# Hybrid encoder layer on one core: loads and stores moved behind the turns, one product moved ahead of some values, the end planned anew

## The chip, the cores and the metric

The kernel runs on one core of one Trainium2 chip. The metric is the time of the whole launch in microseconds, taken on the device. Engines are named as the profile names them: PE is TensorE, PEld its weight loads, DVE VectorE, ACT ScalarE, POOL GpSimd, SP SyncE, which here only issues DMAs. A "q" behind an engine's name (SPq) means its instruction queue: a DMA's row there lasts as long as the queue was held by issuing it, not as long as the transfer.

## What is computed

One encoder layer for 4096 tokens of width 1024, in float32. Cut to what matters:

```python
def reference(x, ...):                       # x: (1, 4096, 1024)
    h = rmsnorm(x, pre_norm_g)
    proj = h @ w_in                          # 1024 -> 2304
    q, k, v, g_a, u_p, g_p = split(proj)     # 8 query heads, 2 key heads of 64
    a = banded_attention(q, k, v, rel_bias, sink) * silu(g_a)
    p = multiscale_pool(u_p, pool_w, pool_scale) * silu(g_p)
    mixed = concatenate([a, p]) @ w_out      # 1024 -> 1024
    return x + rmsnorm(mixed, post_norm_g)

def banded_attention(...):   # blocks of 128 queries, each sees 3 blocks of keys
    s = q . k * scale + bias, masked to |i-j| <= 128
    p = exp(s - m) / (sum(exp(s - m)) + exp(sink - m))
    return p . v
```

## The kernel before

Every float32 number is carried as two float16 (a high part and the rest), so a product of two matrices is three products of halves. Large products are made with seven half-size products in place of eight, and with sums of quarters before and behind them. The names p1 to p7, S1 to S4, s1 to s4 and OT1 to OT4 stand for these.

**First stage** (until about 490 us of the profiled execution). Passes m = 0 to 7 over tiles of 512 tokens. Each makes the gates and the pooling path, and writes to DRAM what the second stage reads: the normed x in halves (`x_scr`), sums of its quarters (`y_scr`), the attention gates (`ga_scr`), the pooled values (`yp_scr`) and weights. `cast` makes a high part on ACT and a rest on DVE. `x_loads` brings the rows of x of a later pass for their squares. `q_pair` folds and scales query weights, with a small matmul for their norm (`pair_norm`).

**Second stage.** 32 blocks b of 128 tokens, in 16 units u of two blocks, run from 31 down to 0. A pass m takes the units ua = 16 - 2m and ub = 15 - 2m, and with them the projections for the units that follow. For each block and each half of its heads:

- `scores` (PE): queries times keys, into the two score banks.
- `softmax`: `logits` (DVE), `exps` (ACT), `sinks`, `denominators` (DVE), `probs` (ACT, the high halves), `rests` (DVE, the low halves into `pn`).
- `turn` (SP): one transposing DMA, `pt<-pn`.
- `values` (PE, function `attend` plans it): probabilities times values. It runs 18 matmuls on the first half of the heads and 18 on the second, each waiting for its own turn.

Between these PE makes the products of the other parts: `do_kv` (keys and values), `q_product` p1 to p7 (queries), and for the output `product` by way of `mix_p1` to `mix_p7`. Behind the output products come `add`, `square`, `gain`, `mean`, `rescale`, then `add_x`, which GpSimd issues as a DMA that adds x in DRAM onto the finished tile `mo`, and `store_sum`, which SP issues as soon as that DMA has landed (`out<-mo`).

**The order is planned.** Each step is put into a list with a due time (`due(t, fn, ...)`), `now[0]` counts PE's time in products, and the list is sorted by due time at the end. The due times thus only set the order in which each engine gets its instructions; each engine then works through its own in that order and waits where it has to. `visit(b, half)` plans the scores and the softmax, with the turn 7.8 us behind the softmax's start (all starts are kept in `starts`). `settled(plan)` goes over the list once more and moves steps on DVE and ACT to places inside a softmax where they do not delay it: its `spans` are (from, to, new place, how many at most), measured from a start. The end, blocks 3 to 0, is written out by hand with times `at_(t, ...)` from z on.

**x in SBUF.** `load_x(m, name)` brings 1 MB into one of three slots. X and W are the two halves of the pass's tokens, Y and Z the sums. W of a pass takes the slot of X, the next pass's X the slot of Y, the next Y the slot of Z, and Z the slot of the pass before's W. X is read by p1, p2 and a `do_kv`, Y by p5 and p6, Z by p3 and p7, W by p4 and a `do_kv`.

One pass m > 1 before the change, in PE's order (8 visits, each with scores; the turns follow some 9 us behind):

```
visit(2ua+1,0)  mix_p5 mix_p1 mix_p3  values(2ua+2)
visit(2ua+1,1)  mix_p2 p1 p6
visit(2ua,0)    p2 mix_p6             values(2ua+1)
visit(2ua,1)    p5 p3 mix_p4 mix_p7
visit(2ub+1,0)  mix_p5 mix_p1 mix_p3  values(2ua)
visit(2ub+1,1)  do_kv(ub-1) mix_p2
visit(2ub,0)    p7 mix_p6 mix_p4      values(2ub+1)
visit(2ub,1)    p4 do_kv(ub-2) mix_p7
```

In the last pass `mix_p4` and what follows stand behind p4.

Of the kernel before, what the change touches and what calls it, by code (L numbers as in the profile page):

```python
# [70 lines left out]
def hybrid_layer(ctx: ExitStack, tc, io, out):  # L71
# [82 lines left out]
    with ExitStack() as actx:  # L154
# [1475 lines left out]

    def settled(entries):
# [5 lines left out]
        for t, n, fn, args in sorted(entries, key=lambda s: s[:2]):  # L1637
            if fn in on_dve + on_act + others:
                spans = ()
                if fn in (gain11, q_join3):  # L1640
# [3 lines left out]
                elif fn is rescale:  # L1644
                    spans = ((-0.6, 6.4, 6.4, 99),)
                elif fn is store_sum:
                    spans = ()
                elif fn in on_act:
                    spans = ((0.75, 3.5, 3.3, 1), (0.75, 6.4, 6.4, 99))
                else:  # L1650
                    spans = ((3.8, 7.0, 7.0, 99),)
# [9 lines left out]
                elif fn in (keep_q, rest_q):  # L1661
                    key = "q"
                elif fn in (keep_kq, rest_kq, q_join, q_join3, q_keep):
# [5 lines left out]
                if fn in (mean, rescale, add_x, store_sum):  # L1669
# [10 lines left out]
                last[key] = t  # L1680
            done.append((t, n, fn, args))
# [81 lines left out]
    def rest_kq(u, half, m, i):  # L1763
        q = q_t[u, half]
        nc.gpsimd.tensor_tensor(out=q[:, 1], in0=kq.pop((m, i)), in1=q[:, 0], op=ALU.subtract)
# [362 lines left out]
    def quads_in(u, t):  # L2128
        due(t, pool_in, u, 0)
        due(t + 8.0, pool_in, u, 1)  # L2130
# [34 lines left out]
    for m in range(1, NM):  # L2165
        ua, ub = NU - 2 * m, NU - 1 - 2 * m
        visit(2 * ua + 1, 0)
        if m > 1:
            due(now[0], load_x, m, "Z")
# [12 lines left out]
        if m > 1:  # L2182
            due(pe(M, q_product, m, "p1", 0), q_keep, m)
# [19 lines left out]
        else:  # L2203
            due(pe(M, q_product, m, "p5", 2), q_join, m, "p5", 1, 2)
# [16 lines left out]
        due(now[0] + 1.0, load_x, m + 1, "X")  # L2221
# [6 lines left out]
        visit(2 * ub + 1, 1)  # L2228
        do_kv(ub - 1, 2, 0.0, 0.7, 1.9)
# [11 lines left out]
        visit(2 * ub, 1)  # L2241
        due(now[0], keep_kq, ub - 1, 1, m, 2)
        due(now[0] + 0.6, rest_kq, ub - 1, 1, m, 2)
        due(now[0] + 2.0, load_x, m + 1, "Y")
# [3 lines left out]
        due(t + 1.3, rest_kq, ub - 1, 0, m, 1)  # L2248
# [4 lines left out]
        else:  # L2253
            mix_p4(ua, 2)


# [49 lines left out]
    at_(26.0, product, 1, "s1", OT1, 1)  # L2306
    at_(28.6, scores, 0, 1)
# [20 lines left out]
    at_(7.0, square, 2, 1, 0)  # L2328
    at_(9.9, square, 2, 1, 1)
    at_(11.5, add, 2, (0, HI), (0, HI), 1)  # L2330
    at_(12.3, square, 2, 0, 1)
# [4 lines left out]
    ending(2, 0, 13.8, 39.4)  # L2336

    cast(5.8, 6.4, 1, "22", a22, G)
    cast(6.4, 10.2, 1, "12", a12, G)
    at_(9.0, begin, 1)  # L2340
    at_(13.7, gate, 2)
    at_(14.4, sum1, 1)
    at_(15.1, sum2, 1)
    at_(15.8, sum3, 1, V)
    at_(16.55, sum4, 1)
    cast(16.6, 18.9, 1, "s2", a11, V)
    cast(18.0, 18.1, 1, "s3", a21, G)
    at_(19.9, gain11, 1)
    at_(20.4, square, 1, 0, 0, 0)
    cast(23.5, 24.2, 1, "s1", a_s1, V)  # L2350
    at_(23.45, add, 1, (0, HI), (0, HI), 1)
    cast(24.8, 25.0, 1, "s4", a12, G)
    at_(27.0, add, 1, (1, HI), (0, HI), 0)
    at_(27.7, add, 1, (1, LO), (1, HI), 2)
    at_(28.5, square, 1, 1, 0)
    at_(28.6, add, 1, (1, HI), (1, HI), 1)
    at_(31.2, square, 1, 1, 1)
    at_(33.7, add, 1, (0, HI), (0, HI), 1)
    at_(35.9, square, 1, 0, 1)
# [6 lines left out]
    cast(24.7, 26.1, 0, "22", a22, G)  # L2366
    cast(34.6, 35.0, 0, "12", a12, G)
    at_(31.5, gate, 1)
    cast(32.2, 32.8, 0, "11", a11, V)
# [94 lines left out]
```

## Time and profile before

| | us |
|---|---|
| median of 3 runs | 1205.16 |
| lowest, highest | 1202.57, 1211.08 |
| profiled execution, its own time | 1197.31 |
| its span | 1195.5 |
| PE / DVE / ACT / POOL busy in it | 1139.4 / 920.7 / 758.4 / 289.4 |
| mean clock granted to PE | 0.989 of full speed |

How its rows are read: a timeline's row is start and duration in us, engine, line, operation, what is written and read, and in brackets the engine's idle time just before it and what ended that. L1817 is `values`, L1531 `scores`, L1613 `turn`, L1736 the query products, L1949 the output products, L1492 the keys' product, L1468 `load_x`, L2024 `store_sum`, L2020 `add_x`, L1996 `load_xr`, L1604 `rests`, L989 the products of the first stage. A row of waits is engine and line, what was waited for, the sum in us, how many times, and the longest. Matmuls are pipelined, so the durations of neighbours overlap by some tenths.

### The profile page before, as it was taken

The page shows a single profiled execution, that of the slowest core. Times are in us where ns is not written, and L with a number is a line of the kernel's source. Part 1 is how long each engine was busy: PE and PEld are TensorE (multiplying, and loading weights), DVE is VectorE, ACT ScalarE, POOL GpSimd, SP SyncE. Part 2 cuts the span into 40 slices and gives each one's busy share as a digit, 9 for nine tenths or more (in the row PEclk, how much of TensorE's full clock was granted, in tenths as well). Part 3 has the DMA queues.
Part 4 walks back from the last instruction along what each step waited for, and adds up shares of the span by engine and source line. Part 5 has one row for each costly group of instructions (what it writes and reads, how often), then busy time and mean ns, then how long its engine had stood idle before and what let it go on. Part 6 is the DMA issues. An engine that isn't in the chain of part 4 may idle for free. (4 is left out here: it accounts for less than half of the span.)

```text
span 1195.5 us, 30463 instructions
## 1 busy us (share of the span) xinstructions
PE 1139.4 (95%) x12528; PEld 843.2 (71%) x12528; DVE 920.7 (77%) x1887; ACT 758.4 (63%) x1696; POOL 289.4 (24%) x273
## 2 busy tenths in 40 slices
PE   6999999899999999999999999998999999979987
PEld 4548888788888888877667666666666766656533
DVE  5887888778778877867878778777777787767875
ACT  5756575756465644265777677775777776766762
POOL 1000000000000000011444344443444444443421
PEclk9999999999999999999999999999999999999989
DMA  9578896877789848899999899999799899997885
GB/s 263 141 247 266 206 287 234 317 256 261 241 280 221 294 151 244 305 274 263 213 217 182 197 215 209 191 211 208 172 210 224 191 199 216 184 180 165 185 202 146
DMA packets 312635, 265.00 MB, mean 222 GB/s; under 512 B 214528, under 2 KB 275584, under 8 KB 303792
## 3 DMA queue, kind: packets, MB, share of 16 engines
q1 hardware_dynamic: 308464, 248.38, 79.0%
q0 software_dynamic: 4032, 14.68, 7.1%
q8 instruction: 98, 1.61, 0.5%
q14 instruction: 41, 0.34, 0.1%
HBM read 132.97 MB, written 79.21 MB: 177 GB/s over the span
## 5 line engine op out<-in xcount | busy, mean ns | idle before, releaser
L989 PEld LDWEIGHTS <-wa 128*128 128x128 f16 x3360 | 329.6, 98 | 49.3 <-issue 10.7
L989 PE MATMUL ch<-xt,wa 128*128 128x256 f16 x1920 | 212.8, 273 | 3.8 <-ACT cbig L1001 2.8
L1560 ACT ACTIVATE p_all<-p_all,nm 128x384 f32<-128x384 f32 (+1 forms) x256 | 152.4, 596 | 41.2 <-DVE nm L1549 41.0
L1604 DVE SCALAR_TENSOR_TENSOR pn<-p_all,rd,pn 128x384 f16<-128x384 f32 (+1 forms) x256 | 143.7, 619 | 36.4 <-ACT pn L1596 35.8
L1949 PE MATMUL ms<-wo,ys 128*128 128x512 f16 x720 | 166.9, 382 | 0.3 <-DVE xt L1991 0.2
L1549 DVE CUSTOM_DVE_ANT_0 p_all<-s,ybig,nsink 128x384 f32<-128x384 f32 (+1 forms) x256 | 155.8, 666 | 2.5 <-PE s L1531 2.2
L1596 ACT ACTIVATE pn<-p_all,rd 128x384 f16<-128x384 f32 (+1 forms) x256 | 134.7, 596 | 33.4 <-issue 14.6
L1949 PEld LDWEIGHTS <-ys 128*128 128x128 f16 x720 | 69.3, 98 | 82.2 <-issue 4.2
L1949 PE MATMUL m<-wo,y 128*128 128x512 f16 x540 | 124.8, 381 | 0.0
L989 PE MATMUL cl<-xt,wa 128*128 128x256 f16 x960 | 108.7, 275 | 5.2 <-DVE u L1014 3.0
L1817 PE MATMUL o<-pt,vv 128*64 128x256 f16 x1128 | 73.0, 281 | 24.0 <-DMA pt<-pn 24.0
L1855 POOL TENSOR_TENSOR y<-yf,y 128x512 f16<-128x512 f32 x30 | 34.8, 1163 | 252.2 <-ACT y L1851 252.2
L1949 PEld LDWEIGHTS <-y 128*128 128x128 f16 x540 | 51.9, 98 | 61.6 <-issue 2.1
L1736 PEld LDWEIGHTS <-raw 128*128 128x128 f16 x864 | 83.2, 98 | 14.1 <-issue 2.5
L210 POOL TENSOR_SCALAR ssq<-ssq 128x4 f32<-128x4 f32 (+1 forms) x11 | 4.9, 446 | 354.3 <-ACT jk L201 348.4
L1817 PEld LDWEIGHTS <-vv 128*64 128x64 f16 x1128 | 61.7, 112 | 38.9 <-issue 38.9
L302 DVE TENSOR_TENSOR xt<-ybig,xt 128x1024 f16<-128x1024 f32 x56 | 67.3, 1220 | 14.2 <-ACT xt L297 14.2
L1736 PE MATMUL aq_p<-xt,raw 128*128 128x256 f16 x672 | 76.9, 273 | 0.0
L1855 POOL TENSOR_TENSOR ys<-at,ys 128x512 f16<-128x512 f32 x29 | 35.3, 1216 | 151.2 <-ACT ys L1851 122.8
L1023 ACT ACTIVATE gp<-cbig,cg 128x256 f32<-128x256 f32 x42 | 19.0, 499 | 75.1 <-DVE cbig L1014 75.1
L1531 PE MATMUL s<-k_all,q 64*32 64x288 f16 (+8 forms) x3432 | 64.6, 271 | 1.6 <-ACT q L1480 0.7
L1986 POOL TENSOR_TENSOR mo<-mo,ybig 128x512 f32<-128x512 f32 x39 | 51.1, 1309 | 57.1 <-ACT jkb L1975 57.1
(206 smaller groups left out, 1938.4 us busy)
## 6 DMA issues: line engine op xcount, KB each, us to landing
x_scr<-xt SPq DMA_DIRECT2D x16, 1024.0 KB, 6.5
xt<-x_scr SPq DMA_DIRECT2D x16, 1024.0 KB
xn<-in_x SPq DMA_DIRECT2D x28, 512.0 KB, 6.6
ybig<-in_xT SPq DMA_DIRECT2D x28, 512.0 KB, 6.4
y_scr<-xt SPq DMA_DIRECT2D x14, 1024.0 KB, 6.8
xt<-y_scr SPq DMA_DIRECT2D x14, 1024.0 KB
mo<-in_x POOLq DMA_DIRECT2D x28, 512.0 KB, 7.1
out<-mo SPq DMA_DIRECT2D x28, 512.0 KB, 3.1
```

What stands on the lines that cost most here:

```text
L302: eng.tensor_tensor(out=o[:, w, 1], in0=y_view(i), in1=o[:, w, 0], op=ALU.subtract)
L989: nc.tensor.matmul(acc[:, c], wa[:, q, wi, slot * HK + k, c * P : (c + 1) * P], x[:, xi, k, :], start=(fresh and n == 0), stop=(n > 3 * 2 ...
L1531: nc.tensor.matmul(s_bank[jj][r0 : r0 + nr, gg, c0:c1], q_t[u, half][a, qi, jj, tl + r0 : tl + r0 + nr], k_all[a, ki, kc : kc + c1 - c0], ...
L1549: nc.vector.tensor_tensor_reduce(out=p_t[b, half][:, hh, :nk], in0=s_t[b, half][jj][:, gg, :nk], in1=bias[:, h, lo : lo + nk], scale=negc[ ...
L1560: nc.scalar.activation(p[:, hh, :nk], p[:, hh, :nk], AF.Exp, bias=nm_t[b, half][:, hh : hh + 1], scale=-1.0, accum_out=den_t[b, half][:, h ...
L1596: nc.scalar.activation(prob_view(b, half)[:, 0, i], p_t[b, half][:, i, :nk], AF.Copy, scale=rd_t[b, half][:, 0, i : i + 1],)
L1604: nc.vector.scalar_tensor_tensor(out=pn4[:, 1, i], in0=p_t[b, half][:, i, :nk], scalar=rd_t[b, half][:, 0, i : i + 1], in1=pn4[:, 0, i], o ...
L1736: nc.tensor.matmul(acc[:, jj], w[:, wi, jj, k, :], x[:, xi, k, :], start=(first and n == 0), stop=(last and n > 3 * 2 * HK - 3), skip_grou ...
L1817: nc.tensor.matmul(o_ps[a, 2 * half : 2 * half + 2], v[:, vi, kt, a], pt[b, half][:, pi, g, :, i, :], start=(n == 0), stop=(n == last),)
L1855: eng.tensor_tensor(out=y[:, :, 1], in0=f(u), in1=y[:, :, 0], op=ALU.subtract)
L1949: nc.tensor.matmul(z_t[u, tag], y[:, k, yi, :], wo[o][:, wi, k, :], start=(n == 0 and acc is None), stop=(n == 3 * HK - 1), skip_group_che ...
L1986: eng.tensor_tensor(out=mo, in0=mo, in1=gpost[:, cs], op=ALU.mult)
```

## The change

In the first stage four due times move. In the second, `p5` goes from behind `visit(2ua,1)` to ahead of `values(2ua+1)` in every pass (in pass 1 followed by a `mix_p6`, which was behind it). `mix_p4(ua,2)` of the last pass goes ahead of `values(2ub+1)`, where the other passes have it. The loads of Z, W and X are asked later, that of Y earlier. `clear` moves what would be asked just ahead of a turn to just behind it. The opening projects the queries before keys and values. In the last pass DVE, not POOL, makes the rests of two query tiles. In the end part nearly all times are new; PE's order there changes in one place (`scores(0,1)` ahead of `s1`).

```diff
 # first stage
-            cast(m + 1, "A21", op(6) + late + 1.1)
+            cast(m + 1, "A21", op(6) + late + (1.1 if m > 1 else 0.5))
...
-                x_loads(m, (t + 3, t + 11.8), (t + 4, t + 12.9), (t + 14, t + 41.0), (t + 15, t + 42.1))
+                x_loads(m, (t + 3, t + 11.8), (t + 4, t + 12.9), (t + 24, t + 41.0), (t + 25, t + 42.1))
...
-            at_(m, d + 21.0, pair_norm, s1)
-            at_(m, d + 21.5, pair_scale, s1)
-            at_(m, d + 22.2, pair_scaled, s1)
+            at_(m, d + 23.0, pair_norm, s1)
+            at_(m, d + 23.5, pair_scale, s1)
+            at_(m, d + 24.2, pair_scaled, s1)
 # the planner
+    def clear(t, room):
+        for s in starts:
+            if s + 7.8 - room < t < s + 7.85:
+                return s + 7.85
+        return t
...
-                if fn in (gain11, q_join3):
+                if fn is gain11:
                     spans = ((0.05, 4.45, 4.45, 1),)
...
+                elif fn is rest_kq and args[-1] is nc.vector:
+                    spans = ((0.05, 4.45, 4.45, 1), (0.05, 7.0, 7.0, 99))[args[1] :]
...
+                    if fn is store_sum:
+                        t = clear(t, 7.0)
...
+            elif fn in (load_x, load_ga, pool_in):
+                t = clear(t, 4.0 if fn is load_x else 1.0)
...
-        due(t + 8.0, pool_in, u, 1)
+        due(t + 10.0, pool_in, u, 1)
 # the opening
-    do_kv(u)
-
-    due(now[0] + 1.0, lambda: nc.scalar.activation(dummy, mhalf, AF.Exp))
-    do_q(u, 0, 0)
-    now[0] += 1.3
+    do_q(u, 0, 2)
+    due(now[0] - 2.0, lambda: nc.scalar.activation(dummy, mhalf, AF.Exp))
+    do_kv(u, 0, 0.0, 0.2, 0.8)
+
     visit(NB - 1, 0)
 # a pass
         visit(2 * ua + 1, 0)
         if m > 1:
-            due(now[0], load_x, m, "Z")
...
         visit(2 * ua + 1, 1)
         mix_p2(ua + 1, 1)
         if m > 1:
+            due(now[0], load_x, m, "Z")
...
         if m > 1:
             mix_p6(ua + 1, 1)
-        else:
-            due(pe(M, q_product, m, "p5", 2), q_join, m, "p5", 1, 2)
+        due(pe(M, q_product, m, "p5", 2), q_join, m, "p5", 1, 2)
+        if m == 1:
+            mix_p6(ua + 1, 0)
         attend(2 * ua + 1)
         due(now[0] + 2.0, load_ga, 2 * ua)
         visit(2 * ua, 1)
-        due(now[0] + 1.0, load_x, m, "W")
-        if m > 1:
-            due(pe(M, q_product, m, "p5", 2), q_join, m, "p5", 1, 2)
-            rest_of_12()
-            mix_p4(ua + 1, 0)
-        else:
-            mix_p6(ua + 1, 1)
-            mix_p4(ua + 1, 0)
-            rest_of_12()
+        due(now[0] + 5.0, load_x, m, "W")
+        rest_of_12()
+        mix_p4(ua + 1, 0)
...
         visit(2 * ub + 1, 0)
-        due(now[0] + 1.0, load_x, m + 1, "X")
...
         visit(2 * ub + 1, 1)
+        due(now[0] + 4.5, load_x, m + 1, "X")
...
         due(t, q_join, m, "p7", 2, 2)
+        due(t + 2.0, load_x, m + 1, "Y")
         mix_p6(ua, 0)
-        if m + 1 < NM:
-            mix_p4(ua, 2)
+        mix_p4(ua, 2)
         attend(2 * ub + 1)
...
-        due(now[0] + 0.6, rest_kq, ub - 1, 1, m, 2)
-        due(now[0] + 2.0, load_x, m + 1, "Y")
+        due(now[0] + 0.6, rest_kq, ub - 1, 1, m, 2, kq_eng)
...
-        else:
-            mix_p4(ua, 2)
 # the end
-    at_(26.0, product, 1, "s1", OT1, 1)
-    at_(28.6, scores, 0, 1)
+    at_(26.0, scores, 0, 1)
+    at_(26.9, product, 1, "s1", OT1, 1)
...
-    soft(1, 0, 6.2, 6.9, 10.6, 11.0, 11.1, 13.6)
-    soft(1, 1, 16.5, 17.2, 20.6, 21.0, 21.1, 23.6)
-    soft(0, 0, 24.9, 25.6, 29.4, 29.5, 29.7, 31.7)
-    soft(0, 1, 31.6, 32.3, 36.5, 36.7, 36.8, 38.8)
+    soft(1, 0, 6.2, 6.9, 10.0, 10.4, 10.5, 13.2)
+    soft(1, 1, 14.6, 15.3, 19.2, 19.8, 19.9, 22.0)
+    soft(0, 0, 22.7, 23.4, 27.3, 27.6, 27.7, 29.9)
+    soft(0, 1, 30.4, 31.1, 34.8, 35.0, 35.1, 37.4)
...
-    at_(11.1, gain, 2, 1, LO, V)
-    at_(11.8, gain, 2, 1, HI, V)
-    ending(2, 1, 10.9, 12.5)
+    at_(38.1, gain, 2, 1, LO, V)
+    at_(38.4, gain, 2, 1, HI, V)
+    ending(2, 1, 39.5, 40.3)
...
-    cast(5.8, 6.4, 1, "22", a22, G)
+    cast(5.8, 12.95, 1, "22", a22, V)
...
-    at_(0.5, load_xr, 1, 1)
-    at_(0.6, load_xr, 1, 0)
+    at_(22.3, load_xr, 1, 1)
+    at_(22.4, load_xr, 1, 0)
...
-    at_(10.4, load_xr, 0, 1)
-    at_(10.5, load_xr, 0, 0)
+    at_(30.2, load_xr, 0, 1)
+    at_(30.3, load_xr, 0, 0)
```

`soft(b, half, tl, te, td, tp, tr, tt)` gives the times of the logits, exps, denominators, probs, rests and the turn; `load_xr` brings 512 KB of x for the last units; V and G are DVE and POOL.

More of the change, by code (lines that the diff above doesn't have):

```diff
@@ L1662, in settled @@
                     key = "q"
+                elif fn is rest_kq and args[-1] is nc.vector:
+                    key = args[:2]
                 elif fn in (keep_kq, rest_kq, q_join, q_join3, q_keep):
@@ L1761, in keep_kq, with rest_kq @@
         nc.scalar.copy(q_tile(u, half)[:, 0], kq[m, i])
-    def rest_kq(u, half, m, i):
+    def rest_kq(u, half, m, i, eng=nc.gpsimd):
         q = q_t[u, half]
-        nc.gpsimd.tensor_tensor(out=q[:, 1], in0=kq.pop((m, i)), in1=q[:, 0], op=ALU.subtract)
+        eng.tensor_tensor(out=q[:, 1], in0=kq.pop((m, i)), in1=q[:, 0], op=ALU.subtract)
     Q_STEPS = {
@@ L2241, in hybrid_layer @@
         visit(2 * ub, 1)
+        kq_eng = nc.vector if m + 1 == NM else nc.gpsimd
         due(now[0], keep_kq, ub - 1, 1, m, 2)
-        due(now[0] + 0.6, rest_kq, ub - 1, 1, m, 2)
-        due(now[0] + 2.0, load_x, m + 1, "Y")
+        due(now[0] + 0.6, rest_kq, ub - 1, 1, m, 2, kq_eng)
         t = pe(M, q_product, m, "p4", 1, "p7")
@@ L2247, in hybrid_layer @@
         due(t + 0.7, keep_kq, ub - 1, 0, m, 1)
-        due(t + 1.3, rest_kq, ub - 1, 0, m, 1)
+        due(t + 1.3, rest_kq, ub - 1, 0, m, 1, kq_eng)
         if m + 1 < NM:
@@ L2327, in hybrid_layer @@
     at_(5.3, add, 2, (1, HI), (1, HI), 1)
[L2328 to L2331, printed above, removed]
-    at_(11.1, gain, 2, 1, LO, V)
-    at_(11.8, gain, 2, 1, HI, V)
-    ending(2, 1, 10.9, 12.5)
-    at_(38.7, gain, 2, 0, HI, V)
-    ending(2, 0, 13.8, 39.4)
-    cast(5.8, 6.4, 1, "22", a22, G)
[L2339 to L2359, printed above, removed]
+    at_(12.9, square, 2, 1, 0)
+    at_(13.6, square, 2, 1, 1)
+    at_(13.4, add, 2, (0, HI), (0, HI), 1)
+    at_(14.3, square, 2, 0, 1)
+    at_(38.1, gain, 2, 1, LO, V)
+    at_(38.4, gain, 2, 1, HI, V)
+    ending(2, 1, 39.5, 40.3)
+    at_(38.7, gain, 2, 0, HI, V)
+    ending(2, 0, 39.6, 41.2)
+    cast(5.8, 12.95, 1, "22", a22, V)
+    cast(14.9, 15.0, 1, "12", a12, G)
+    at_(9.6, begin, 1)
+    at_(13.8, gate, 2)
+    at_(17.1, sum1, 1)
+    at_(17.8, sum2, 1)
+    at_(18.4, sum3, 1, V)
+    at_(22.7, sum4, 1)
+    cast(18.4, 18.6, 1, "s2", a11, V)
+    cast(18.7, 18.9, 1, "s3", a21, V)
+    at_(19.85, gain11, 1)
+    at_(19.15, square, 1, 0, 0, 0)
+    cast(22.3, 22.9, 1, "s1", a_s1, G)
+    at_(25.3, add, 1, (0, HI), (0, HI), 1)
+    cast(26.05, 26.3, 1, "s4", a12, G)
+    at_(26.1, add, 1, (1, HI), (0, HI), 0)
+    at_(26.8, add, 1, (1, LO), (1, HI), 2)
+    at_(29.7, square, 1, 1, 0)
+    at_(29.7, add, 1, (1, HI), (1, HI), 1)
+    at_(33.7, square, 1, 1, 1)
+    at_(34.2, add, 1, (0, HI), (0, HI), 1)
+    at_(37.3, square, 1, 0, 1)
     at_(40.7, gain, 1, 1, LO, V)
@@ L2364, in hybrid_layer @@
     ending(1, 0, 40.1, 44.1)
[L2366 to L2369, printed above, removed]
+    cast(26.4, 30.6, 0, "22", a22, G)
+    cast(34.6, 37.5, 0, "12", a12, G)
+    at_(33.0, gate, 1)
+    cast(33.8, 37.6, 0, "11", a11, V)
     at_(45.9, gate, 0)
```

## The prediction

> **What bounds the kernel now.** I read the page first, then what TensorE waits for in the second stage, then the timelines of TensorE and of the DMA queue on SyncE there.
>
> ```profile
> span 1195.5 us, 30463 instructions
> PE 1139.4 (95%) x12528; PEld 843.2 (71%) x12528; DVE 920.7 (77%) x1887; ACT 758.4 (63%) x1696; POOL 289.4 (24%) x273
> ```
>
> TensorE is busy for 95% of the span and the change takes no product away, so it can only gain what TensorE loses in waits and in slow clock. The waits of TensorE from 500 us to the end:
>
> ```profile
> PE o L1817 <- DMA pt<-pn: 24.0, 12, 6.8
> PE s L1531 <- ACT q L1480: 0.7, 1, 0.7
> ...
> PE s L1531 <- DVE q L1483: 0.4, 1, 0.4
> ```
>
> Nearly all of it is one thing, 24.0 us in 12 waits: `values` of a block waits for the turned probabilities of its second half. The longest of these waits, with what follows two of them:
>
> ```profile
> 566.01 2.13 PE L1817 MATMUL o<-pt,vv 128*64 128x256 f16 x18 [2.50 <-DMA pt<-pn]
> ...
> 818.53 2.13 PE L1817 MATMUL o<-pt,vv 128*64 128x256 f16 x18 [3.26 <-DMA pt<-pn]
> ...
> 1074.72 2.13 PE L1817 MATMUL o<-pt,vv 128*64 128x256 f16 x18 [6.78 <-DMA pt<-pn]
> ...
> 1137.76 1.17 PE L1817 MATMUL o<-pt,vv 128*64 128x256 f16 x18 [1.87 <-DMA pt<-pn]
> ...
> 1161.47 1.17 PE L1817 MATMUL o<-pt,vv 128*64 128x256 f16 x18 [3.70 <-DMA pt<-pn]
> 1162.58 4.45 PE L1949 MATMUL ms<-wo,ys 128*128 128x512 f16 x12
> ```
>
> The first three are `values(2ua+1)` in passes m = 1, 4 and 7. The last two belong to the end. The other seven waits share 24.0 - 18.1 = 5.9 us. Three of them are `values(2ua+1)` again (m = 2, 5, 6), two `values(2ub+1)`, two lie in the opening. I give half of the 5.9, 3.0, to `values(2ua+1)`. So that one place costs 2.50 + 3.26 + 6.78 + 3.0 = 15.5 us. After each of its three long waits 18 matmuls take 2.13 us where 1.17 is normal: 3 x 0.96 = 2.9 us more. At stake there: 18.4 us.
>
> Why just there? The view of the turned tile gives the time from asking to landing:
>
> ```profile
> DMA to landing us min/median/max: 4.3/7.2/9.2
> ```
>
> Pass m = 4, TensorE and then SyncE's queue:
>
> ```profile
> 798.88 0.93 PE L1531 MATMUL s<-k_all,q 64*32 64x288 f16 x48
> ...
> 811.41 2.75 PE L1949 MATMUL ms<-wo,ys 128*128 128x512 f16 x12
> ...
> 820.59 1.53 PE L1531 MATMUL s<-k_all,q 64*32 64x256 f16 x96
> ...
> 843.65 1.19 PE L1531 MATMUL s<-k_all,q 64*32 64x128 f16 x96
> 844.77 2.79 PE L1492 MATMUL kv<-xt,raw 128*128 128x256 f16 x24
> ...
> 867.11 2.78 PE L1492 MATMUL kv<-xt,raw 128*128 128x256 f16 x24
> ```
>
> ```profile
> 808.06 5.37 SPq L1613 DMA_TRANSPOSE pt<-pn  x1
> ...
> 829.83 4.27 SPq L1613 DMA_TRANSPOSE pt<-pn  x1
> 834.20 0.53 SPq L1468 DMA_DIRECT2D xt<-x_scr  x1
> ...
> 853.47 4.08 SPq L1613 DMA_TRANSPOSE pt<-pn  x1
> ...
> 869.60 0.42 SPq L1468 DMA_DIRECT2D xt<-y_scr  x1
> 872.02 6.72 SPq L1613 DMA_TRANSPOSE pt<-pn  x1
> ```
>
> The scores at 798.88 lead to a turn at 808.06, 9.2 us later. TensorE wanted its result at 818.53 - 3.26 = 815.3, only 7.2 us after that: the median landing, with no room. The turn at 829.83 had until about 842.6 (the second half of the `values` that end at 843.65), 12.7 us.
>
> **The change part by part.** *One more product.* `q_product p5` moves from behind `visit(2ua,1)` to ahead of `values(2ua+1)`; at m = 1 `mix_p6` goes ahead too. A product is 2.7 us (811.41). That removes the three short waits (3.0), the 2.50 and its 0.96, leaves 0.6 of the 3.26, and 4.1 of the 6.78 with its 0.96: 18.4 - 5.6 = 12.8 us saved. At m = 1 the product put ahead needs `s2`, whose rest GpSimd makes at the place quoted next:
>
> ```profile
> 562.58 1.16 POOL L1855 TENSOR_TENSOR ys<-at,ys 128x512 f16<-128x512 f32 x1 [27.29 <-ACT ys L1851]
> ```
>
> It ends at 563.74; TensorE is there at 566.01 - 2.50 - 1.17 = 562.34. A new wait of 1.4 us. On the other side `values(2ua)` comes 2.7 us nearer to its turn: 12.7 us less 2.7 is 10.0, over the longest landing of 9.2: 0.
>
> By the Trainium skill (TensorE: Matmul & The Clock Gate, "What's actually happening") the clock falls to half after an idle window of about 3.4 us, which would leave the waits of 2.50 and 3.26 without a slow stretch and make this saving 1.9 us smaller; the rows of 2.13 us behind both show that it fell here, though the page says that the window runs free.
>
> *Loads and stores behind the turns.* Before, a store of a finished block (`out<-mo`) stands ahead of a turn in SyncE's queue and waits for the accumulating load that GpSimd asked for:
>
> ```profile
> SPq L2024 <- DMA mo<-in_x: 147.4, 27, 7.9
> ```
>
> ```profile
> 1061.82 0.34 SPq L2024 DMA_DIRECT2D out<-mo  x1
> 1062.26 7.19 SPq L1613 DMA_TRANSPOSE pt<-pn  x1
> ...
> 1074.49 0.34 SPq L2024 DMA_DIRECT2D out<-mo  x1
> ```
>
> That turn is the one of the 6.78 us wait. `clear` puts such stores, and load_x within 4 us of a turn, just behind it. A turn on the queue takes 6.72 us with a 1 MB load 2.4 us ahead (872.02) and 4.08 without (853.47). The turns of `visit(2ua,1)` and `visit(2ub,1)` lose such a load, but their values do not wait: 0. What does wait is `visit(2ua+1,1)`, and it gets a new neighbour: from m = 2 on, Z is asked after `mix_p2`, some 802.3 on this pass's clock, 5.7 us ahead of the turn at 808.06. A 1 MB load lands in 6.5 us:
>
> ```profile
> mo<-in_x POOLq DMA_DIRECT2D x28, 512.0 KB, 7.1
> ...
> wo<-w_scr SPq DMA_DIRECT2D x8, 1024.0 KB, 6.5
> ```
>
> They overlap for 0.8 us, where the load of 869.60 overlapped its turn for 4.1 us and cost 2.6. By proportion that is 0.5 us each, and it counts only at m = 4 and 7, where no room is left: 1.0. (Bounds: 0, and 2.6 in each of six passes.)
>
> *Loads that are now late.* A turn holds SyncE's queue until its last rest is made, and for the 4 to 7 us of its own issue; what now stands behind it waits for both. W is asked behind the turn of `visit(2ua,1)`: 829.83 + 4.27, as the load at 834.20 was, landing at about 840.7. Its reader, the kv product of `visit(2ub+1,1)` (844.77), comes at 842.1, as one product has left. Margin 1.4 us: 0. The next X is asked behind the turn at 853.47 + 4.08 and a store, at 858.0, landing at 864.5 for the kv product at 867.11. If it shares the engines with the accumulating load (7.1 us for half the bytes), 1.5 MB at the same rate take 9.75 us, 0.6 us too late. I take 0.3 in six passes: 2 lost. (Bounds: 0, and the case priced under the rivals.) Y moves earlier, its slot being free after p7, and has its next reader a pass later: 0. The stores leave later by one turn, and their buffers are next written over half a pass later: 0.
>
> *The opening.* `do_q` before `do_kv` puts 5 us of kv products between the query projection and the first scores. The waits of 0.7 and 0.4 go: 1.1 saved (at worst 0).
>
> *The end.* The soft steps are planned earlier and the residual loads leave the turns:
>
> ```profile
> 1127.18 1.62 SPq L1996 DMA_DIRECT2D raw<-in_x  x2
> 1128.91 6.57 SPq L1613 DMA_TRANSPOSE pt<-pn  x1
> ...
> 1152.35 5.45 SPq L1613 DMA_TRANSPOSE pt<-pn  x1
> ```
>
> `values(2)` loses a product ahead of it (`mix_p4` goes before `values(2ub+1)`, 2.7 us), and its turn loses the loads (6.57 against 4.08): 0. For `values(1)` the turn is planned 1.6 us earlier, and from 1152.35 to 1161.47 it took 9.1 us, where 7.2 is the median: 1.9. Together 3.5 us saved. Bounds: 1.87 + 3.70 + 1.7 (the product of 4.45 us against 2.75) = 7.3 saved, 2.7 lost.
>
> `rest_kq` on VectorE in the last pass, q_join3's new place and `gain` moved later shift work on engines with 23% and more of the span idle: 0, unless VectorE is late for a turn, which the end's bound takes in.
>
> *First stage.* The planned times of four steps move:
>
> ```profile
> 151.93 1.23 DVE L302 TENSOR_TENSOR xt<-ybig,xt 128x1024 f16<-128x1024 f32 x1 [0.78 <-ACT xt L297]
> ```
>
> ```profile
> 153.81 4.42 PE L989 MATMUL ch<-xt,wa 128*128 128x256 f16 x39 [0.96 <-DVE u L1014]
> ```
>
> ```profile
> 235.26 2.78 PE L989 MATMUL ch<-xt,wa 128*128 128x256 f16 x24 [2.55 <-ACT cbig L1001]
> 238.78 0.38 PE L426 MATMUL n<-wsq,ones 128*128 128x2 f32 x2 [0.74 <-ACT wj L422]
> ```
>
> A21's cast 0.6 us earlier goes ahead of the gates on ScalarE and takes 0.78 out of VectorE's way to the join that TensorE waits for. `pair_norm` 2 us later takes 0.74. Together 1.5. The later x loads free the queue; the 2.55 us wait of 235.26 bounds that, either way; I take 0.
>
> **The sum.** 12.8 - 1.4 - 1.0 (room in steady passes) - 2 (X) + 1.1 + 3.5 + 1.5 = 14.5 us. The profiled execution took 1197.31 us (span 1195.5), so 1182.8. The median of the runs, 1205.16, lies 7.85 higher. The span does not show why. I assume waits of the same kind, half of which the added room takes: 1182.8 + 4 = 1187.
>
> **Rivals.** *Z eats the room.* If Z delays each turn of `visit(2ua+1,1)` by the full 2.6 us from m = 2 on, the extra product is given back there and only m = 1 keeps about 1 us: the saving falls from 14.5 by some 9.5 to 5, 1200. For it: it is the one turn with no room, and the load stands ahead of it. Against: 5.7 us is most of a load's 6.5. The Trainium skill (DMA: Bandwidth & Descriptors, "Queues, rings and completion order") says that a DMA's completion is counted only after every earlier write of the same DMA engine, whatever the queue, which is this rival's mechanism. The store at 1074.49, which waits for the accumulating load, and the wait that ended at 1074.72 fit it without proving it.
>
> *Loads late: slower.* W and the next X, in one place, the kv products. Their margins are 1.4 and 2.6 us. Each us beyond these is a wait of TensorE, 13 times (seven W, six X). If every load comes 2.5 us late, 32.5 us are lost against 16.5 saved: 1205 + 16 = 1221. It decides from 16.5 / 13 = 1.3 us late each. For it: no load is asked earlier than a turn allows, and a turn's time on the queue goes up to 7.19 us. Against: a turn without a load ahead took 4.1 to 4.3, and W then runs alone.
>
> *The long wait is not of the order.* The 6.78 us may be chance: other runs would then have less to save there, 7 us less, 1194. It lies inside the range.
>
> **Chances.** Forecast 0.65 (its own range 1175 to 1194), Z 0.24, loads late 0.11. The range must hold 8 in 10: from 1171 (the end's full 7.3 and the whole offset gained) to 1207, which takes in the Z case. About 1% is what a measurement of this kernel can tell from no change. Faster by over 1% (under 1193): 0.65. Within 1%: 0.24. Slower by over 1%: 0.11.
>
> **What would show it.** Right: `o<-pt` waits fall from 24.0 to under 10 us, with none over 1 us at `values(2ua+1)` but chance ones; no TensorE wait of kv on `xt<-x_scr`; no `out<-mo` wait directly ahead of a turn; the first scores without a wait. Wrong: waits of kv products on `xt<-x_scr` (loads late), `values(2ua+1)` still waiting in most passes with turns of over 6 us on the queue (Z), new waits on VectorE in the last 70 us.

## The result, and the profile after

| | before | after |
|---|---|---|
| median, us | 1203.87 (4 runs) | 1168.97 (4 runs) |
| lowest to highest | 1197.85 to 1211.08 | 1167.71 to 1169.97 |
| ratio, 95% interval | | 0.971 [0.965, 0.976] |
| profiled execution, span | 1197.31, 1195.5 | 1169.97, 1168.2 |

The change made the kernel 35 us faster, more than twice the 14.5 us of the sum, and the runs lie within 2.3 us of each other where those of before lie 13 apart. The time lies 2 us below the range's lower end. All figures here and below are of fast executions; a slower state of the chip showed in one of the ten of `near_stores` and in two of the kernel before beside it. First the two lines of the page (span, busy times) and then what TensorE waits for from 490 us to the end, in the changed kernel. Its lines are numbered a little higher: L1831 is `values`, L1963 the output products, L1750 the query products, L2038 `store_sum`, L2034 `add_x`.

```profile
span 1168.2 us, 30455 instructions
PE 1132.3 (97%) x12528; PEld 839.2 (72%) x12528; DVE 920.6 (79%) x1890; ACT 757.4 (65%) x1696; POOL 286.5 (25%) x270
```

```profile
PE o L1831 <- DMA pt<-pn: 1.7, 3, 0.9
PE aq L1750 <- DVE q L1483: 1.1, 1, 1.1
PE s L1531 <- ACT k_all L1480: 1.0, 2, 0.5
PE kv L1492 <- DMA xt<-x_scr: 1.0, 3, 0.5
...
PE ms L1963 <- POOL ys L1869: 0.6, 1, 0.6
PE ms L1963 <- ACT ys L1865: 0.5, 1, 0.5
```

The one large row of before, 24.0 us in 12 waits for `pt`, is 1.7 in 3. Two small new ones are as forecast: `kv` on the next X, and pass 1's product on `s2` (the last two rows, 1.1 us together). The 1.1 us on a query tile (`aq` on `q`) lie in the opening and were not forecast. TensorE's busy time fell by 7 us as well, and its mean granted clock rose from 0.989 to 0.998: there are fewer slow stretches behind waits. And in SyncE's queue the stores wait for almost nothing: 147.4 us in 27 before, here

```profile
SPq L2038 <- DMA mo<-in_x: 8.0, 2, 4.6
```

### The profile page after: what moved, and what is told of

It reads as the page before. It is cut to its first block, busy times and chain, and to the rows that moved or that the text cites. A ratio compares the mean times of both kernels' runs of the same rounds, so it can differ in the third digit from the quotient of the medians.

```text
span 1168.2 us, 30455 instructions
## 1 busy us (share of the span) xinstructions
PE 1132.3 (97%) x12528; PEld 839.2 (72%) x12528; DVE 920.6 (79%) x1890; ACT 757.4 (65%) x1696; POOL 286.5 (25%) x270
## 4 chain that ended last, share of the span: by engine, by line
PE 43%; DMA 4%; DVE 3%; ACT 1%; issue 1%; SPq 0%; DVEq 0%; POOLq 0%; ACTq 0%
PE ms L1963 11%; PE aq_p L1750 9%; PE m L1963 8%; PE o L1831 4%; PE s L1531 4%; PE kv L1492 3%; PE kv L1712 3%; DMA xt<-x_scr 2%; DMA pt<-pn 2%; PE z L1935 1%; DVE pn L1604 1%; DVE p_all L1549 1%; PE s L1935 0%; DVE mo L2005 0%; SPq L1613 0%
## 5 line engine op out<-in xcount | busy, mean ns | idle before, releaser
L1963 PE MATMUL ms<-wo,ys 128*128 128x512 f16 x720 | 165.4, 379 | 3.0 <-DVE ys L1869 0.8
L1963 PEld LDWEIGHTS <-ys 128*128 128x128 f16 x720 | 68.8, 98 | 84.0 <-issue 2.4
L1963 PE MATMUL m<-wo,y 128*128 128x512 f16 x540 | 124.0, 379 | 0.3 <-DVE mo L2005 0.2
L1750 PEld LDWEIGHTS <-raw 128*128 128x128 f16 x864 | 83.3, 98 | 17.4 <-issue 4.8
L1963 PEld LDWEIGHTS <-y 128*128 128x128 f16 x540 | 51.6, 98 | 61.4 <-issue 1.5
L1750 PE MATMUL aq_p<-xt,raw 128*128 128x256 f16 x672 | 78.1, 273 | 0.4 <-issue 0.4
L1831 PE MATMUL o<-pt,vv 128*64 128x256 f16 x1128 | 68.4, 274 | 1.8 <-DMA pt<-pn 1.7
L1831 PEld LDWEIGHTS <-vv 128*64 128x64 f16 x1128 | 59.2, 110 | 14.3 <-issue 14.3
L1531 PE MATMUL s<-k_all,q 64*32 64x288 f16 (+7 forms) x3432 | 63.1, 265 | 1.5 <-ACT k_all L1480 1.0
```

The source lines that it names most:

```text
L1531: nc.tensor.matmul(s_bank[jj][r0 : r0 + nr, gg, c0:c1], q_t[u, half][a, qi, jj, tl + r0 : tl + r0 + nr], k_all[a, ki, kc : kc + c1 - c0], ...
L1750: nc.tensor.matmul(acc[:, jj], w[:, wi, jj, k, :], x[:, xi, k, :], start=(first and n == 0), stop=(last and n > 3 * 2 * HK - 3), skip_grou ...
L1831: nc.tensor.matmul(o_ps[a, 2 * half : 2 * half + 2], v[:, vi, kt, a], pt[b, half][:, pi, g, :, i, :], start=(n == 0), stop=(n == last),)
L1963: nc.tensor.matmul(z_t[u, tag], y[:, k, yi, :], wo[o][:, wi, k, :], start=(n == 0 and acc is None), stop=(n == 3 * HK - 1), skip_group_che ...
```

## The experiments

Differences are given against 1168.4, the middle of the changed kernel's two medians (1168.97, and 1167.85 beside the last runs), or against the kernel before as measured beside the run. The two medians lie 1.1 us apart, so a difference of a us or two says little by itself.

### Four parts taken back, one at a time

`u_p5`: the extra product.

```diff
-        due(pe(M, q_product, m, "p5", 2), q_join, m, "p5", 1, 2)
-        if m == 1:
-            mix_p6(ua + 1, 0)
         attend(2 * ua + 1)
...
         visit(2 * ua, 1)
+        due(pe(M, q_product, m, "p5", 2), q_join, m, "p5", 1, 2)
```

> The changed kernel with the extra product ahead of values(2ua+1) taken back (q_product p5 behind visit(2ua,1) again, and at m = 1 mix_p6 too); all the rest of the change stays. Theory (room: a turn needs 7 to 9 us and had 7.2): the waits of values(2ua+1) come back in nearly every pass, 18.4 us with their slow stretches, less the 1.2 us that the product put ahead waits at m = 1: 1169 + 17 = 1186. Rival (order: the long wait of 6.78 us came from a waiting store ahead of the turn, and is gone with it): only 18.4 - 7.7 come back, less 1.2: 1169 + 9.5 = 1178.5. If neither: under 1174.

Measured 1176.68 (1176.07 to 1177.89), 8.3 us slower: near the rival's 1178.5 and far from 1186. The long wait does not come back:

```profile
PE o L1831 <- DMA pt<-pn: 10.1, 7, 4.2
```

The longest, 4.2 us, is in pass 1, ahead of which no store stands.

`u_order`: all loads and stores in the order of before.

```diff
-                    if fn is store_sum:
-                        t = clear(t, 7.0)
...
-            elif fn in (load_x, load_ga, pool_in):
-                t = clear(t, 4.0 if fn is load_x else 1.0)
...
-        due(now[0] + 5.0, load_x, m, "W")
+        due(now[0] + 1.0, load_x, m, "W")
```

(and X, Y, Z and `pool_in` likewise.)

> The changed kernel with the order of all loads and stores (X, Y, Z, W, the shares of the accumulating loads, the quads, the stores) as before; the extra product, the end and the first stage stay changed. Theory (order matters for the long wait): a store that waits for the accumulating load stands ahead of a turn again, a wait of 4 us (6.78 less one product) comes back in one or two passes with a slow stretch of 1 us, the three waits of kv for the next X (1.0 us) go: 1172 to 1178, and the runs spread by several us as those of before did (13 us). Rival (room is all): 1168 to 1170, spread under 3 us.

Measured 1178.99, and the four runs lie from 1174.33 to 1191.64: 10.6 us slower, and the spread of before is back, though each `values(2ua+1)` has its extra product. The profile is that of the execution of 1191.64, the slowest of the four; it has two long waits, of 9.5 and 8.8 us where some 4 were expected. Its waits for `pt`, and the last `rests`, SyncE's queue, GpSimd's and the transfers at the longest of them:

```profile
PE o L1827 <- DMA pt<-pn: 19.9, 5, 9.5
```

```profile
635.39 2.20 DVE L1604 SCALAR_TENSOR_TENSOR pn<-p_all,rd,pn 128x384 f16<-128x384 f32 x4
```

```profile
638.65 0.34 SPq L2034 DMA_DIRECT2D out<-mo  x1
639.10 13.58 SPq L1613 DMA_TRANSPOSE pt<-pn  x1
...
655.41 0.34 SPq L2034 DMA_DIRECT2D out<-mo  x1
```

```profile
639.80 0.90 POOL L2030 DMA_DIRECT2D mo<-in_x  x1
...
mo<-in_x POOLq DMA_DIRECT2D x1, 512.0 KB, 15.6
```

Read in order of time: the store of one finished block waits until an accumulating load has landed (638.6). The turn stands behind it and was ready at 637.6 (635.39 + 2.20), so it starts 1.5 us late, at 639.10. At 639.80 GpSimd asks for the next accumulating load. Store, turn and load now run at once, and at least two of them crawl: the turn holds the queue for 13.58 us, the load lands after 15.6 (7.1 is its median before). When the store landed is not in the trace. The same is in the profile of before at its 6.78 us wait: store 1061.82, turn 1062.26, and

```profile
1062.96 0.88 POOL L2020 DMA_DIRECT2D mo<-in_x  x1
```

`u_end`: the end (and the last pass's `mix_p4` and `kq_eng`) planned as before.

```diff
-    soft(1, 1, 14.6, 15.3, 19.2, 19.8, 19.9, 22.0)
+    soft(1, 1, 16.5, 17.2, 20.6, 21.0, 21.1, 23.6)
...
-    at_(30.2, load_xr, 0, 1)
+    at_(10.4, load_xr, 0, 1)
```

> The changed kernel with the end planned as before (soft steps, order of the last scores and product, residual loads, rest_kq of the last pass on GpSimd, mix_p4 of the last pass behind the last visit). By the forecast's term: 3.5 us slower than the changed kernel, 1172.5. By the difference of the two traces from the last scores of m = 7 on: 6.3 us or more, 1175.5. From values(1) and values(2) waiting: 3.70 and 1.87 us in the trace again, and the product behind with 4.45 us.

Measured 1177.71 (1176.58 to 1179.62), 9.3 us slower: far over the forecast's 3.5, and in keeping with the "6.3 us or more". TensorE's long waits of the end in it, and SyncE's turn of `values(1)`:

```profile
1121.99 0.50 PE L1531 MATMUL s<-k_all,q 64*128 64x256 f16 x6 [2.38 <-DVE nm L1549]
...
1140.29 2.13 PE L1827 MATMUL o<-pt,vv 128*64 128x256 f16 x18 [5.17 <-DMA pt<-pn]
```

```profile
1124.67 0.47 SPq L1888 DMA_DIRECT2D yf<-yp_scr  x1
1125.23 0.38 SPq L2041 DMA_DIRECT2D wo<-w_scr  x1
1125.71 0.39 SPq L2034 DMA_DIRECT2D out<-mo  x1
1128.92 7.76 SPq L1613 DMA_TRANSPOSE pt<-pn  x1
```

In the changed kernel the same two places:

```profile
1130.28 0.50 PE L1531 MATMUL s<-k_all,q 64*128 64x256 f16 x6 [0.43 <-DVE nm L1549]
...
1135.59 1.17 PE L1831 MATMUL o<-pt,vv 128*64 128x256 f16 x18 [0.66 <-DMA pt<-pn]
```

```profile
1128.39 3.66 SPq L1613 DMA_TRANSPOSE pt<-pn  x1
1132.10 1.05 SPq L2010 DMA_DIRECT2D raw<-in_x  x2
```

With nothing asked for in the 4.9 us ahead of it the turn holds the queue for 3.66 us in place of 7.76, and the residual loads go behind it. The wait for the turn is 4.5 us shorter. The scores' wait on VectorE (2.38) has no row in the quoted waits of before: with that end it appears when TensorE arrives earlier.

`u_first`: the three edits of the first stage taken back.

```diff
-            cast(m + 1, "A21", op(6) + late + (1.1 if m > 1 else 0.5))
+            cast(m + 1, "A21", op(6) + late + 1.1)
...
-                x_loads(m, (t + 3, t + 11.8), (t + 4, t + 12.9), (t + 24, t + 41.0), (t + 25, t + 42.1))
+                x_loads(m, (t + 3, t + 11.8), (t + 4, t + 12.9), (t + 14, t + 41.0), (t + 15, t + 42.1))
...
-            at_(m, d + 23.0, pair_norm, s1)
+            at_(m, d + 21.0, pair_norm, s1)
```

> The changed kernel with the first stage as before (cast A21, x loads, pair_norm). By the forecast's term: 1.5 us slower than the changed kernel, 1170.5. By the two traces: 4.3 us slower, 1173.3, with TensorE reaching the second stage at 495 instead of 491 us, and a wait of 2.2 us on VectorE's u at about 319 us there again.

Measured 1174.30 (1172.46 to 1176.00), 5.9 us slower. It is split up further down.

### Stores, loads, and nearness

`u_stores` takes back only the move of the stores, `u_loads` only those of X, Y, Z, W, and of the gates and pooled values (`load_ga`, `pool_in`; the expectations call them shares and quads). `near` is the changed kernel with one due time moved, so that GpSimd asks for the second accumulating load 0.9 us behind the turn in place of 2.14, with no store ahead. `near_stores` is both, nearness and the stores ahead.

```diff
 # u_stores
-                    if fn is store_sum:
-                        t = clear(t, 7.0)
 # u_loads
-            elif fn in (load_x, load_ga, pool_in):
-                t = clear(t, 4.0 if fn is load_x else 1.0)
 # and load_x Z, W, X, Y and pool_in at the places of before
 # near, and near_stores (which has the first edit too)
-        due(t + 4.2, sum3, u)
+        due(t + 4.9, sum3, u)
```

> The changed kernel with the stores of finished blocks planned as before (ahead of the turns again); loads, product, end and first stage stay changed. Theory (held turn): a store that waits for the first accumulating load holds a turn of visit(2ua+1,1) by about 1.5 us where that load takes 9 us, the turn then starts only 0.6 to 0.7 us ahead of the second accumulating load instead of 2.1, and both crawl (turn 12 to 17 us, load 11 to 16): a wait of 5 to 9 us in one or two passes, 1174 to 1180, with runs 5 us or more apart. Rival (the moved loads did it): no turn over 10 us, 1168 to 1171, runs within 3 us.

> The changed kernel with X, Y, Z, W, the shares and the quads asked for at the places of before; the stores stay behind the turns. Theory (held turn, by the stores alone): no turn of visit(2ua+1,1) takes over 10 us, no wait of over 2 us at its values, runs within 3 us, and the three waits of kv for X (1.0 us) go: 1167 to 1170. Rival (loads): crawling turns and a median of 1174 or more.

> The changed kernel with one thing moved on GpSimd: the subtraction sum3 is planned 0.7 us later, so that the second accumulating load of each pass is asked for ahead of it, 0.9 us behind the turn of visit(2ua+1,1) instead of 2.14. No store stands ahead of a turn. Theory (nearness alone makes both crawl): turns of 12 to 17 us in each of the passes m = 2 to 7, 5 to 9 us of wait in each: 1200 to 1220. Rival A (nearness only together with a first accumulating load of 9 us): in the passes with such a load (two to four): 1178 to 1200. Rival B (a distance of 0.9 is far enough, or it is the store's wait itself): 1167 to 1171.

> The changed kernel with both: the stores ahead of the turns as before, and the second accumulating load of each pass asked for 0.9 us behind the turn of visit(2ua+1,1), as in the run before with the load near (which alone left turns of 3.7 to 5.6 us on the queue and 1170). Theory (three at once: the 512 KB store, the turn and the accumulating load within some 1.5 us make all three crawl): turns that land after 9 to 17 us in most passes m = 2 to 7, waits at values(2ua+1) of 2 to 9 us in each, 1185 or more. Rival A (a turn crawls only where the first accumulating load takes 9 us and the store holds it): long turns in the same one or two passes as without the nearness, 1174 to 1180. Rival B (chance): waits under 2 us, 1172 or less.

| run | median (lowest to highest) | against 1168.4 |
|---|---|---|
| `u_stores` | 1176.50 (1174.98 to 1178.80) | +8.1 |
| `u_loads` | 1166.42 (1163.94 to 1167.33) | -2.0 |
| `near` | 1169.97 (1165.66 to 1170.32) | +1.6 |
| `near_stores` | 1218.25 (1211.65 to 1220.32) | +49.9 |

Nearness alone costs next to nothing: my theory that it makes both crawl fell with `near`. The store ahead alone costs 8. Both together cost 50, five times their sum, and make the kernel slower than before (ratio 1.013 [1.009, 1.016] to it). The waits of 5 to 9 us and the runs 5 us apart that were expected of `u_stores` did not come (more on that below). The waits for `pt` in `near`, then in `near_stores`, and the queues and transfers of the latter in pass 2:

```profile
PE o L1831 <- DMA pt<-pn: 3.2, 4, 1.2
```

```profile
PE o L1829 <- DMA pt<-pn: 37.2, 9, 9.4
```

```profile
646.38 0.34 SPq L2036 DMA_DIRECT2D out<-mo  x1
647.44 6.18 SPq L1613 DMA_TRANSPOSE pt<-pn  x1
```

```profile
648.36 0.90 POOL L2032 DMA_DIRECT2D mo<-in_x  x1
```

```profile
DMA  9989999805999999979986699974349987864100
GB/s 400 455 337 419 394 315 129 41 9 109 289 290 264 196 120 61 35 31 26 122 42 61 49 59 96 113 28 24 11 34 91 110 158 151 199 171 178 55 23 5
...
mo<-in_x POOLq DMA_DIRECT2D x1, 512.0 KB, 16.0
```

```profile
664.55 1.86 PE L1829 MATMUL o<-pt,vv 128*64 128x256 f16 x15 [7.12 <-DMA pt<-pn]
```

Here the store did not hold the turn; it only ran beside it. The two rows of tenths and GB/s are 40 slices of 647 to 665 us: the DMA engines stay busy for most of it, but in the middle they move under 130 GB/s, often under 50, where they began at 400. So it is neither the store's wait nor the nearness of the load alone; it is store, turn and accumulating load together. What in the DMA engines makes them slow is not shown.

Nor is it shown what decides how slow. The profile of `u_stores` has two such meetings, in passes 2 and 7, with the load asked for 0.77 and 0.87 us behind the turn. The second, in SyncE's queue and in TensorE's:

```profile
1051.75 0.34 SPq L2036 DMA_DIRECT2D out<-mo  x1
1052.19 6.37 SPq L1613 DMA_TRANSPOSE pt<-pn  x1
```

```profile
1063.99 1.17 PE L1829 MATMUL o<-pt,vv 128*64 128x256 f16 x18 [3.33 <-DMA pt<-pn]
```

The turns held the queue for 5.20 and 6.37 us, the loads landed after 9.6 and 10.7, and `values` waited 1.94 and 3.33 us: slower than without the store, but far from the 13.58 and 15.6 of `u_order`. And the runs of `u_stores` lie only 3.8 us apart.

### Alone on the kernel before

`a_order` is the new order of loads and stores on the kernel before, `a_stores` the move of the stores alone, `clear` as quoted in the change and its one call:

```diff
 # both
+                    if fn is store_sum:
+                        t = clear(t, 7.0)
 # a_order alone, with load_x Z, W, X, Y and pool_in at the new places
+            elif fn in (load_x, load_ga, pool_in):
+                t = clear(t, 4.0 if fn is load_x else 1.0)
```

> The kernel before with the new order of loads and stores alone (no further product, end and first stage as before). Theory (order): the wait of 6.78 us and its slow stretch go, the waits of 1 to 3 us for the turned tile stay; by the reverse experiment about 10 us faster than before, 1193 to 1198, and runs within 4 us where those of before spread over 13. By the forecast's terms (room lost to Z 1.0, X late 2.0): 1206 to 1209. Rival (the run-to-run spread has another source): spread of 10 us or more.

> The kernel before with one edit alone: a store of a finished block that is planned within 7 us ahead of a turn goes behind it. Theory (three at once was the long wait and the spread): no turn over 10 us at values(2ua+1), the 6.78 us wait goes, the short waits for room stay; 1190 to 1194, runs within 5 us. If the moved loads had a share in the gain of the whole order (1191.2): 1197 or more.

`a_order`: 1191.23 (1187.85 to 1193.64) beside 1206.93, 15.7 us faster: more than the 10 expected, with runs 5.8 us apart where 4 were. `a_stores`: 1186.75 (1185.19 to 1187.70) beside 1204.56, 17.8 us faster, ratio 0.986 [0.982, 0.990]: half of the whole gain from one rule for the stores, and its runs lie within 2.5 us. Its waits for `pt`, and the turn of pass 4 that had no room before:

```profile
PE o L1825 <- DMA pt<-pn: 11.8, 7, 5.0
```

```profile
810.13 4.35 SPq L1613 DMA_TRANSPOSE pt<-pn  x1
...
814.59 0.52 SPq L2032 DMA_DIRECT2D out<-mo  x1
```

```profile
817.73 1.17 PE L1825 MATMUL o<-pt,vv 128*64 128x256 f16 x18 [0.23 <-DMA pt<-pn]
```

The turn held the queue for 5.37 us at this place before, with the store 0.44 us ahead. With the store behind it is 4.35. From the turn to `values` it took 10.5 us (808.06 to 818.53) and now takes 7.6 (810.13 to 817.73), and the wait of 3.26 us is 0.23, with no product added. What stays are pass 1 (5.0, where it was 2.50; no store stands there, and why it grew is not shown), the end (3.65) and 3.1 us in five short waits.

The moved loads work against this. The waits for `pt` in passes 2 to 7 alone (600 to 1100 us), in `u_p5` and `a_order`, which have the moved loads and no further product, and in `a_stores`, which has neither:

```profile
PE o L1831 <- DMA pt<-pn: 5.2, 5, 1.7
```

```profile
PE o L1827 <- DMA pt<-pn: 5.9, 5, 1.7
```

```profile
PE o L1825 <- DMA pt<-pn: 0.9, 3, 0.4
```

All these are at `values(2ua+1)`. In pass 7 of `u_p5` Z is asked for 7 us ahead of its turn, and the turn holds the queue for 4.42 us; in `a_stores`, without Z there, for 3.67. That Z does it is likely; no run moves it alone without the product.

### The first stage

`f_xl`, `f_cast` and `f_pn` each take back one of the three edits quoted with `u_first`: the x loads, the cast, `pair_norm` with the two steps behind it.

> The changed kernel with only the x loads of the first stage at their times of before (10 us earlier). The forecast gave this edit 0, the whole first stage 1.5; measured was 5.4 for the whole (TensorE reaches the second stage at 495.4 us in the mean of three profiles of the old first stage, at 490.0 in seven of the new). Theory (the x loads stand ahead of something that the join waits for): 2 to 4 us slower than the changed kernel, 1171 to 1173, second stage at 492 to 494, with VectorE's u late by 1 to 2 us near 319 us. Rival (A21 or pair_norm): 1168 to 1170.

> The changed kernel with only the cast A21 of c = 1 at its time of before (0.6 us later). By the forecast's term: about 0.8 us slower than the changed kernel, with the wait of 0.95 us on VectorE's u at 154 us there again; 1170. Rival (it is what makes the first stage gain more): 1171 to 1173.

> The changed kernel with only pair_norm and the two steps behind it at their times of before (2 us earlier). By the forecast's term: 0.7 us slower than the changed kernel, with the wait of 0.74 us on ScalarE's wj at about 239 us again and waits on u at 261 and 319 us back if these were ScalarE's order: 1170 to 1172. Rival (the move of c = 0 costs what the others gain, 0.34 and 1.03 us at 176 us): the same as the changed kernel.

Measured 1174.24, 1169.32 and 1167.93: +5.8, +0.9 and -0.5. The x loads are nearly the whole of it, and more than the 2 to 4 us expected. The wait of 0.74 us on `wj` is back in `f_pn`, yet the kernel is no slower: the rival's outcome. VectorE and then TensorE near 319 us with the early x loads (`f_xl`):

```profile
305.65 1.23 DVE L291 TENSOR_TENSOR ybig<-ybig,rb 128x1024 f32<-128x1024 f32 x1 [1.52 <-DMA ybig<-in_xT]
307.43 1.23 DVE L291 TENSOR_TENSOR ybig<-ybig,rb 128x1024 f32<-128x1024 f32 x1 [0.55 <-DMA ybig<-in_xT]
```

```profile
319.53 9.69 PE L989 MATMUL cl<-xt,wa 128*128 128x256 f16 x72 [2.45 <-DVE u L1014]
```

and in the changed kernel:

```profile
303.02 2.35 DVE L291 TENSOR_TENSOR ybig<-ybig,rb 128x1024 f32<-128x1024 f32 x2
```

```profile
316.25 8.02 PE L989 MATMUL cl<-xt,wa 128*128 128x256 f16 x72 [0.20 <-DVE u L1014]
```

SyncE's queue there, first with the early x loads, then in the changed kernel:

```profile
289.99 2.23 SPq L261 DMA_DIRECT2D xn<-in_x  x2
...
299.42 2.60 SPq L281 DMA_DIRECT2D ybig<-in_xT  x2
```

```profile
295.42 1.85 SPq L281 DMA_DIRECT2D ybig<-in_xT  x2
297.32 0.99 SPq L261 DMA_DIRECT2D xn<-in_x  x2
```

Two loads of rows that are only wanted later (for their squares) stood ahead of the two transposed loads that VectorE needs for the tile. Ahead of them, `ybig` is asked for 4 us earlier (1 us of it because the run with the early loads was that much late already; 1.7 us because SyncE there waited, by the profile, for an `xn` load to land), VectorE no longer waits for it, and its join `u` comes in time for TensorE.

### What is left on the table

`u_z` puts only Z back; `best` is the changed kernel without the moved loads and without the moved `pair_norm`; `after2` is the changed kernel once more, on the same chip.

```diff
 # u_z
         visit(2 * ua + 1, 0)
         if m > 1:
+            due(now[0], load_x, m, "Z")
...
         mix_p2(ua + 1, 1)
         if m > 1:
-            due(now[0], load_x, m, "Z")
 # best: the edit of u_loads, and
-            at_(m, d + 23.0, pair_norm, s1)
+            at_(m, d + 21.0, pair_norm, s1)
```

> The changed kernel with only Z asked for at its old place (ahead of mix_p5 instead of behind mix_p2). By the forecast's term the new place costs 0.5 us in two passes: 1168. If Z is what makes the moved loads cost 2.6 us in sum: 1166.5. If it is the late X and W: 1169, with the three waits of kv for X (1.0 us) still there.

> The changed kernel without the moved loads (X, Y, Z, W, shares and quads at their places of before) and without the moved pair_norm; the stores, the extra product, the end, the later x loads and the cast stay. Theory (moved loads cost 2 to 3 us, pair_norm 0 to 1): 1165 to 1167, 2 to 3 us faster than the changed kernel. Rival (chips and runs differ by as much): 1168 to 1170.

> The changed kernel itself once more, beside the others on one chip. 1168 to 1170 as in its first runs. If it comes out at 1166 or less, the moved loads cost nothing and the difference to the runs without them was the chip's.

Measured 1167.87, 1165.92 (1164.96 to 1166.73) and 1167.85 (1167.60 to 1170.28). `best` beats the changed kernel by 1.9 us, and its highest time lies below the lowest of `after2`, as that of `u_loads` does below the lowest of all the changed kernel's runs. So the moved loads cost about 2 us (the move of `pair_norm` is in `best`'s figure too), and with the product ahead Z has no share in it. In the profile of `best` TensorE has no wait on X; in the changed kernel the next X is on its chain of waits, in pass 6:

```profile
1011.38 9.56 DMA xt<-x_scr
1020.99 2.79 PE kv L1492 x24
```

Its 9.56 us are close to the 9.75 of the estimate.

## Why the prediction was wrong

**Direction and place were right, the main mechanism was not**, and the size was 18 us off (1187 against 1169). Step by step:

- *Stores behind the turns: 0.* This is the step that failed by most. The prediction quoted the store ahead of the 6.78 us wait and said that it leaves later at no cost, but gave its leaving no gain. It was worth 17.8 alone on the kernel before, and 8.1 at the end of all the others.
- *"The median landing, with no room", one more product 12.8 saved.* The place was right, the reason mostly not. From pass 2 on the turns of `values(2ua+1)` were late because the store ran beside them, more than for want of room: with the stores alone moved, the waits there fall from 13.0 us (1.29, 3.26, 0.20, 1.47, 6.78) to 0.9. The view's 4.3 to 9.2 us was read as what such a turn takes; but from the turns at 808.06 and 1062.26 to their `values` (818.53 and 1074.72) it took 10.5 and 12.5 us, over the view's longest, so it can't have been theirs. The product was worth 8.3: in pass 1 3.3 of wait (4.20 without it, 0.87 with it) and a slow stretch of 1.0, and in the passes from 2 on the 5.2 of wait that the moved loads bring, less 1.1 for `s2`. Without the moved loads it would be worth some 4 us, by estimate from these figures (8.3 - 5.2 + 0.9).
- *Of the 6.78, 4.1 left.* Nothing of it is left, but not by the product: where a turn crawls, a product does not cover it. In `u_order`, with the product, the waits were 9.5 and 8.8.
- *The offset of 7.85, half of it taken.* All of it went: the profiled execution of the changed kernel (1169.97) lies 1.0 over its median. The spread of 13 us went too; it is 2.5 in `a_stores` and 17.3 with the whole old order back, but 3.8 with the stores alone put back, so the stores are not shown to be its only source. That the slower runs hold more crawls is likely, but only one execution of each kernel was profiled.
- *Z 1.0 lost, X late 2.0 lost.* Together 3.0; measured about 2, of which 1.0 is seen: `kv` waits 1.0 us on X in three passes. W never is late, and Z costs nothing with the product ahead (`u_z`).
- *Pass 1 loses 1.4 on `s2`:* 1.1, right.
- *Opening 1.1:* from TensorE's start of the stage to the first scores of pass 1 it took 48.73 us before (495.08 to 543.81) and 47.83 after (490.81 to 538.64), 0.9 less. The figure is right partly by luck: the waits of 0.7 and 0.4 went, but one of 0.5 on the keys and one of 1.1 on a query tile came, and one of 1.4 on turned probabilities, which the forecast did not count there, went.
- *The end 3.5, at most 7.3:* 9.3. The bound counted the two waits at their length of before, but not that VectorE would have been late for the scores by 2.4 and 0.7 us, which showed only once TensorE came earlier, nor that the wait for the turn of `values(1)` would then be 5.2 in place of 3.70.
- *First stage 1.5, x loads 0:* 5.9, nearly all from the x loads; of the two terms of the 1.5 only the cast's showed (0.9, with its wait of 1.0 us back in `f_cast`). The x loads were bounded by the wait of 2.55 on `cbig`, which stayed (2.35). The 2.19 on `u` at 319 us, whose chain leads to loads queued behind the x loads, was left out.
- *The range from 1171.* Its lower end was worked out wrongly: 1182.8 already has the whole offset out of it, and 1171 takes the 7.85 off once more. By its terms it is 1179 (1182.8, less the 3.8 by which the end's 7.3 exceeds its 3.5), so the result lies 10 us beyond what they allow.

Of the rivals, Z did not eat the room that the product gives, though the moved loads do lengthen that turn where there is no product. The loads were late by under 0.5 us where the slower case needed 1.3. "The 6.78 us may be chance" was half true: its size differs from run to run, but its cause stands in the order of the queue.

## What to carry over

A transfer that runs beside a transposing DMA makes it slower, so a measured landing time holds only for its company: before buying room for a late transfer with work put ahead, look at what is asked for in the 2 us before and behind it, and move that. A prefetch asked for too early costs time too (5.8 us here), if a load that is wanted now stands behind it in the queue. Where runs of one kernel differ by a per cent, a meeting of transfers that is long in some runs only may be the reason; here its removal was worth more (17.8 us) than the waits that went from the profiled run (24.0 - 11.8 = 12.2).

## What was not expected of the hardware

A 512 KB store, a transposing DMA and a 512 KB accumulating load asked for within 2 us (`near_stores`, pass 2): the load took 16.0 us where 7.1 is its median before, and the rate fell from 400 GB/s to under 50 while the DMA engines stayed busy. Other such meetings were milder: in `u_stores` the load landed after 9.6 and 10.7 us. Without the store ahead (`near`) loads 0.9 us behind a turn landed after 8.3 to 10.3 us; with the store ahead and the load 2.1 us behind the turn (`u_stores`, the passes whose turn was not held) after 7.0 to 8.4.
